# Output projection and gate as two passes over pairs of blocks, seven half-size products in place of eight

## The chip, the cores and the metric

The kernel runs as one program on one core of one Trainium2 chip. The metric is device time in microseconds (us), from the launch of the program to its end on that core; the kernel before takes 2761.39 us (median of three runs, 2760.68 to 2761.46). The names of the engines are those of the profile: PE is TensorE (PEld its weight loads), DVE is VectorE, ACT is ScalarE, POOL is GpSimd, and SP is SyncE, which only issues DMA transfers here.

## The reference, cut to what matters

One layer is computed for 2048 prompt tokens and for 64 sample tokens (8 sequences of 8), all in float32:

```python
xn   = rmsnorm(h, norm_mix)
proj = xn @ w_in + b_in                      # (tokens, 1024) @ (1024, 9 * 1024)
q, fz, iv, za, ga, gb, zb, ma, mb = split(proj)
o, s_new = hgrn2(silu(q), f(fz), iv, s0)     # recurrence with a 128 x 128 state for each of 8 heads
y_a  = (rmsnorm(o) * silu(za)) @ w_br_a
cv   = silu(layernorm(depthwise_conv31(ga * sigmoid(gb))))
y_b  = (cv * silu(zb)) @ w_br_b
merged = sigmoid(ma) * y_a + sigmoid(mb) * y_b
h    = h + merged @ w_o                                   # output projection
gate = sigmoid(rmsnorm(h, norm_ple) @ w_ple_gate)         # gate
h    = h + gate * (p_l @ w_ple)
y    = rmsnorm(h, norm_final)
```

The new recurrent states and the last 30 convolution inputs are outputs too. The change concerns mostly the four lines from `h = h + merged @ w_o` on. Both `w_o` and `w_ple_gate` are 1024 x 1024.

## The kernel before, in words

Each float32 matrix product is made of three products in a rounded type (`F32R`): an operand is split into a high part `hi`, which ACT makes with a copy into that type, and a low part `lo`, which DVE makes as `x - hi`; PE then adds up hi\*hi, hi\*lo and lo\*hi in PSUM. A tile of work for PE is one matmul with a 128 x 128 stationary operand and up to 512 moving columns.

There are three stages. The first (up to about 1980 us) goes head by head over two halves of the sequence: for each head the nine slices of `w_in` are multiplied by the transposed input (line 1374), and between those products PE works off the small matmuls of the recurrence. In the second half the sample tokens are a tail of the second prompt group. For each head, `sample_state` (line 611) multiplies the 64 transposed sample keys by a masked 64 x 1024 copy of the values `vm` in two matmuls of 512 columns in plain float32 (line 613), eight states of 128 x 128 in all. The second stage (about 1980 to 2324 us) is the two branch products, `w_br_a` and `w_br_b`, with the layer norm of the convolution between them on DVE, ACT and POOL. In these two stages an order written out by due times decides: `at_time(t, fn, prio)` puts a step behind the unit of PE work in whose time `t` falls; a unit is one product of 512 columns or less, with 24 matmuls.

The third stage (from about 2324 us) has no due times, only the order of the calls at the end of the kernel. It works block by block, 128 tokens each, 16 prompt blocks and one of 64 sample tokens (class `Out`, line 1163). For a block, `load_m` and `split_m` bring the transposed `merged` block and split it; `out_proj` (line 1215) makes two products of 24 matmuls (8 slices of the contraction times 3), adds the residual, squares and sums; `rstd` runs three short POOL instructions; DVE scales the block into `hs`; `turn` (line 1241) transposes it on PE and splits it; `gate` (line 1264) makes two products of 24 matmuls with `w_ple_gate` and two of 6 matmuls with `w_ple`, takes the sigmoid, multiplies, adds to `h`, squares again, and `L1287` scales the finished block, which ACT's queue stores. All matmuls of this stage are on line 1203, in `gemm`. The sample block packs its high and low parts side by side in the 128 stationary columns and so needs two matmuls where the others need three.

Both weights lie in SBUF split into high and low parts, `w_o` prepared by 16 loads and splits in the last part of the second stage, one half of `w_ple_gate` there too, the other half between the first blocks of the third stage. The call order is software-pipelined: `turn` of block b, `out_proj` of b+1, `split_m` of b+2, `gate` of b. The residual block `h` has three buffers; its load (line 1190) waits on SP until the output store of an older block has read its buffer, and the loads that are issued behind it on SP, `mgr` (line 1176) and `p` (line 1195), wait with it. This stage has eight PSUM buffers (`ps3`).

At the start, `x_load` brings the first two 128-token blocks, then the norm weights `nmix`, then the first weight slice; `x_norm` squares on ACT, computes the factor on POOL, and scales on DVE (line 166); `x_turn` transposes on PE (line 178) and splits.

## Time and profile before

| what | value |
|---|---|
| median of three runs | 2761.39 us |
| the profiled execution: time of the run, span from first to last instruction | 2761.78 us, 2760.0 us |
| mean granted TensorE clock | 0.999 |
| PE busy | 2735.6 us, 99% of the span |
| DVE, ACT, POOL busy | 1937.9, 928.7, 280.5 us |
| the chain that ended last, by engine | PE 95%, DVE 2%, DMA 1% |
| third stage, 2324 to 2760 us: PE, DVE, ACT, POOL busy | 427.12, 180.54, 133.52, 31.86 us |

The table is read from top to bottom: first whether the clock was full, then which engine was busy nearly all the time, then whether the chain that ended last agrees with it. A busy PE is not a PE at its peak, since the recorded durations of matmuls overlap: a matmul of 512 columns lasts about 390 ns in the records, but the next one starts 227 ns after it. The spacing is what counts in a sum.

### The profile page before, as it was taken

To read this page: it belongs to the slowest core of one execution; us is meant where nothing else is said; L and a number is where in the kernel's file an instruction comes from. 1 tells how busy PE (TensorE), PEld (TensorE's weight loads), DVE (VectorE), ACT (ScalarE), POOL (GpSimd) and SP (SyncE) were. 2 spreads that over 40 slices of the span, in tenths; PEclk is the share of its full clock that TensorE was granted. 3 is DMA by queue.
4 is the path that set the end of the run, shared out by engine and by line. 5 is a ranking of instruction groups with operands and counts; after the bars stand their busy time and mean duration, and the time that the engine had idled before them with its cause. 6 is when DMAs were issued, how large, how long until landed. Compare 5 with 4: busy or idle time off the path is not lost.

```text
span 2760.0 us, 50577 instructions
## 1 busy us (share of the span) xinstructions
PE 2735.6 (99%) x21199; PEld 2354.0 (85%) x21199; DVE 1937.9 (70%) x3219; ACT 928.7 (34%) x2096; POOL 280.5 (10%) x441
## 2 busy tenths in 40 slices
PE   8999999999999999999999999999999999999998
PEld 6888888888888898989889898989889888888887
DVE  6577877877768887686878778787977765444433
ACT  5333333333333423323233333233244332323322
POOL 2001000000000000010000000000036410000000
PEclk9999999999999999999999999999999999999999
DMA  4222222222222422121222222223687776322211
GB/s 125 62 73 81 76 82 81 88 89 68 75 66 65 131 69 82 58 81 58 77 73 80 70 65 77 62 86 103 193 274 219 235 249 212 102 71 70 71 50 40
DMA packets 330252, 275.37 MB, mean 100 GB/s; under 512 B 16474, under 2 KB 281787, under 8 KB 330024
## 3 DMA queue, kind: packets, MB, share of 16 engines
q1 hardware_dynamic: 265552, 192.44, 23.3%
q10 hardware_dynamic: 64200, 79.51, 8.4%
q8 instruction: 166, 2.72, 0.4%
q14 instruction: 62, 0.51, 0.1%
q0 software_dynamic: 272, 0.19, 0.0%
HBM read 192.60 MB, written 79.49 MB: 99 GB/s over the span
## 4 chain that ended last, share of the span: by engine, by line
PE 95%; DVE 2%; DMA 1%; ACT 0%; issue 0%; POOL 0%; DVEq 0%; POOLq 0%; SPq 0%; ACTq 0%
PE mm L1374 71%; PE ps L1203 14%; PE d32p L468 1%; PE ab L476 1%; PE o L565 1%; PE kv L538 1%; PE o L567 1%; DVE acc L717 1%; PE kvs L613 1%; PE vtr L401 1%; PE pt L1254 0%; PE ktr L526 0%; PE otr L591 0%; DMA raw<-in_w_br_a_dram 0%; PE d32p L454 0%; PE ab L468 0%
## 5 line engine op out<-in xcount | busy, mean ns | idle before, releaser
L717 DVE SCALAR_TENSOR_TENSOR acc<-u,cw,acc 128x512 f32<-128x512 f32 x960 | 743.5, 774 | 20.7
L1374 PE MATMUL mm<-x1h,whi 128*128 128x320 f32 (+2 forms) x2112 | 705.5, 334 | 0.0
L1374 PE MATMUL mm<-x1h,wlo 128*128 128x320 f32 (+2 forms) x2112 | 688.4, 326 | 0.0
L1374 PE MATMUL mm<-x1l,whi 128*128 128x320 f32 (+2 forms) x2112 | 688.1, 326 | 0.0
L1374 PE MATMUL mm<-x0h,whi 128*128 128x512 f32 (+1 forms) x1416 | 562.9, 398 | 0.4 <-ACT x0h L181 0.4
L1374 PE MATMUL mm<-x0l,whi 128*128 128x512 f32 (+1 forms) x1416 | 551.8, 390 | 1.5 <-DVE x0l L182 1.3
L1374 PE MATMUL mm<-x0h,wlo 128*128 128x512 f32 (+1 forms) x1416 | 551.7, 390 | 0.0
L1374 PEld LDWEIGHTS mm<-x1h,whi 128*128 128x128 f32 x2112 | 397.4, 188 | 33.8 <-ACT rp L382 4.5
L1374 PEld LDWEIGHTS mm<-x1h,wlo 128*128 128x128 f32 x2112 | 397.3, 188 | 28.2
L1374 PEld LDWEIGHTS mm<-x1l,whi 128*128 128x128 f32 x2112 | 397.1, 188 | 26.3
L333 DVE TENSOR_TENSOR wlo<-raw,whi 128x1024 fp32r<-128x1024 f32 x176 | 216.3, 1230 | 216.0 <-ACT whi L332 209.9
L1374 PEld LDWEIGHTS mm<-x0h,wlo 128*128 128x128 f32 x1416 | 266.5, 188 | 56.9 <-DVE wlo L333 0.4
L1374 PEld LDWEIGHTS mm<-x0h,whi 128*128 128x128 f32 x1416 | 267.1, 189 | 55.0 <-issue 1.2
L1374 PEld LDWEIGHTS mm<-x0l,whi 128*128 128x128 f32 x1416 | 267.0, 189 | 52.8 <-DVE x0l L182 2.2
L332 ACT ACTIVATE whi<-raw 128x1024 fp32r<-128x1024 f32 x176 | 186.1, 1057 | 101.2 <-DVE mal L909 34.3
L1203 PE MATMUL ps<-woh,mgi 128*128 128x512 f32 x528 | 168.4, 393 | 0.5 <-DVE mgi L1185 0.5
L429 DVE TENSOR_TENSOR rp<-rp 128x512 f32<-128x512 f32 (+1 forms) x224 | 156.7, 700 | 9.6
L442 DVE TENSOR_TENSOR lvl<-kq,rp 128x512 f32<-128x512 f32 (+2 forms) x224 | 146.6, 654 | 1.9
L1203 PEld LDWEIGHTS ps<-woh,mgi 128*128 128x128 f32 x528 | 99.1, 188 | 21.3 <-DVE mgi L1185 1.0
L800 ACT ACTIVATE sp<-mm,vcol 128x512 f32<-128x512 f32 (+2 forms) x120 | 73.0, 609 | 127.9 <-PE mm L1374 116.0
L576 POOL TENSOR_SCALAR ors<-oss 128x4 f32<-128x4 f32 (+1 forms) x40 | 11.1, 276 | 970.2 <-ACT on L574 970.2
L1203 PE MATMUL ps<-wol,mgi 128*128 128x512 f32 x272 | 106.1, 390 | 0.0
(253 smaller groups left out, 3153.0 us busy)
## 6 DMA issues: line engine op xcount, KB each, us to landing
raw<-in_w_in_dram SPq DMA_DIRECT2D x144, 512.0 KB, 4.0
gate<-am_dr SPq DMA_DIRECT2D x24, 512.0 KB, 5.0
xt<-in_x_prompt_dram SPq DMA_DIRECT2D x16, 512.0 KB, 5.0
g_dr<-gst ACTq DMA_DIRECT2D x32, 256.0 KB, 2.8
cv_dr<-acc ACTq DMA_DIRECT2D x32, 256.0 KB, 2.2
raw<-in_w_br_a_dram SPq DMA_DIRECT2D x16, 512.0 KB, 5.4
raw<-in_w_br_b_dram SPq DMA_DIRECT2D x16, 512.0 KB, 6.7
mgr<-mg_dr SPq DMA_DIRECT2D x16, 512.0 KB, 4.9
```

The lines of the kernel that those rows point to most:

```text
L332: nc.scalar.activation(out=b.hi, in_=b.raw, func=AF.Copy)
L333: nc.vector.tensor_tensor(out=b.lo, in0=b.raw, in1=f32(b.hi), op=ALU.subtract)
L401: nc.tensor.transpose(pt[:, P * c:P * (c + 1)], self.vt[:, P * c:P * (c + 1)], ident)
L429: nc.vector.tensor_tensor(out=io, in0=io, in1=tt, op=ALU.mult)
L442: nc.vector.tensor_tensor(out=o, in0=a, in1=b, op=ALU.mult)
L468: nc.tensor.matmul(dst[32 * b:32 * b + 32, c, s:s + 16], lhsT=kk[:, o:o + 32], rhs=lv[:, o:o + 32].rearrange("p (a e i) -> p a e i", e=2, ...
L476: nc.tensor.matmul(self.ab[o:o + h, c, o + h:o + 2 * h], lhsT=lv[:, P * c + o:P * c + o + h], rhs=lv[:, P * c + o + h:P * c + o + 2 * h], ...
L538: nc.tensor.matmul(self.kv[:, c, :], lhsT=self.kt[:, c, :], rhs=self.v[:, c, :], start=True, stop=True)
L717: nc.vector.scalar_tensor_tensor(out=self.acc, in0=self.u[:, i:i + G], scalar=w, in1=self.acc, op0=ALU.mult, op1=ALU.add)
L800: nc.scalar.activation(out=s[:, 0:n], in_=ps[:, 0:n], func=func, bias=bias(kind, j))
L1203: nc.tensor.matmul(ps, lhsT=a[:, k, :], rhs=c[:, k, s], start=(k == 0 and i == 0), stop=(k == kn - 1 and i == len(ops) - 1))
L1374: nc.tensor.matmul(ps[:, 0:u.n], lhsT=w[:, k, :], rhs=x[:, k, sl], start=(k == 0 and w is u.block.hi and x is xh), stop=(k == KB - 1 and w ...
```

## The change

The two 1024 x 1024 products of the third stage are computed from quarters. Two blocks form a pair, so that the left operand is a 2 x 2 grid of (128 tokens) x (512 of the contraction), the weight a 2 x 2 grid of 512 x 512 quarters, and the result a 2 x 2 grid of (128 tokens) x (512 columns). Seven products of 12 matmuls each (4 slices of the contraction times 3), over sums of quarters, replace the eight quarter products; the sums of the left side are made per pair, and their results are recombined. Because the gate's weights take the place of the output projection's in SBUF, the stage becomes two passes over eight pairs: the first stores `h` and the transposed normed block to DRAM (`h_dr`, `t_dr`), the second loads both. The `w_ple` products and all transposes keep their number. The sample tokens are handled once in each pass, behind the fourth pair, from the same quarters: 40 matmuls in place of 32 in the output projection, and 40 as before in the gate, with 8 for `w_ple`.

Sums of weight quarters are formed in the second stage by POOL (16 loads, 16 subtractions and 16 stores of 128 x 512 for each weight) and kept in DRAM (`ts_dr`). In the first stage the sample state is computed from rows of 32, and at the start `nmix` is loaded ahead of the second block.

```diff
 # start
     x_load(0)
+    nc.sync.dma_start(out=nmix, in_=norm_mix...)
     x_load(1)
-    nc.sync.dma_start(out=nmix, in_=norm_mix...)
...
-    x_norm(0)
-    x_norm(1)
+    x_stat(0)
+    x_stat(1)
+    x_scale(0)
+    split_hi(blocks[0])
+    x_scale(1)
...
 # sample state: vm is now 128 x 2 x 128, made by DVE from a transposed copy of the values in row tiles
         def sample_state(self, e):
-            kv = ps_1.tile([P, 4, P], F32, tag="kv", name="kvs")
-            nc.tensor.matmul(kv..., lhsT=self.kts, rhs=self.vm[:, 4 * e:4 * e + 4, :]..., start=True, stop=True)
-            s0 = self.s0[:, 4 * e:4 * e + 4, :]
-            nc.vector.tensor_tensor(out=s0, in0=s0, in1=kv, op=ALU.add)
+            kvs = [ps_1.tile([P, 4, P], F32, tag=tag, name="kvs") for tag in ("kv", "ab")]
+            for i, kv in enumerate(kvs):
+                r = slice(64 * e + 32 * i, 64 * e + 32 * i + 32)
+                nc.tensor.matmul(kv[:, 0:2, :], lhsT=self.kts[r], rhs=self.vm[r], start=True, stop=True)
+            for i, kv in enumerate(kvs):
+                s0 = self.s0[:, 4 * e + 2 * i:4 * e + 2 * i + 2, :]
+                nc.vector.tensor_tensor(out=s0, in0=s0, in1=kv[:, 0:2, :], op=ALU.add)
...
 # second stage: sums of weight quarters
+    def sums_load(w, k):
+        for op in QUARTERS:
+            sums[w, k, op] = t = p2["sb"].tile([P, G], F32, tag="ts", name="ts", bufs=8)
+            nc.sync.dma_start(out=t, in_=w_src(w, op, k))
+    def sums_make(w, k, i):
+        nc.gpsimd.tensor_tensor(out=out, in0=a, in1=b, op=ALU.subtract)
+        store(w_src(w, op, k), out, 1)
...
 # third stage
+    PRODUCTS = (("a11", "b11"), ("s2", "t2"), ("a12", "b21"), ("s3", "t3"), ("s1", "t1"), ("a22", "t4"), ("s4", "b22"))
+        def add(self, op):          # s1 to s4, sums of left quarters; s1, s3, s4 share one buffer
+            nc.gpsimd.tensor_tensor(out=out, in0=a, in1=b, op=f)
+        def split(self, op):
+            nc.scalar.activation(out=hi, in_=src, func=AF.Copy)
+            nc.vector.tensor_tensor(out=lo, in0=src, in1=f32(hi), op=ALU.subtract)
+        def product(self, i):       # 12 matmuls
+            for k in range(4):
+                for j, (a, b) in enumerate(((ah, bh), (ah, bl), (al, bh))):
+                    nc.tensor.matmul(ps, lhsT=a[:, k, :], rhs=b[:, k, :], ...)
+        def more(self, r, e, t):
+            nc.gpsimd.tensor_tensor(out=self.part(r, e), in0=self.part(r, e), in1=t, op=ALU.add)
+        def scale(self, r):
+            rs = rstd(self.ss[r], P)
+            nc.scalar.dma_start(out=h_dr[b * P:(b + 1) * P], in_=self.h[r])
+            nc.vector.tensor_scalar(out=self.hs[r], in0=self.h[r], scalar1=rs, scalar2=None, op0=ALU.mult)
+        def gate_sum(self, r, e, d, u):
+            nc.vector.tensor_tensor(out=g, in0=self.ps[d], in1=u, op=ALU.add)
+            nc.scalar.activation(out=g, in_=g, func=AF.Sigmoid)
+        def gate_use(self, r, e):
+            nc.vector.tensor_tensor(out=g, in0=self.pp[r, e], in1=g, op=ALU.mult)
+            nc.vector.tensor_tensor(out=h, in0=g, in1=h, op=ALU.add)
+            self.square(r, e, g)
+        def finish(self, r):
+            rs = rstd(self.ss[r], P)
+            nc.vector.scalar_tensor_tensor(out=h, in0=h, scalar=rs, in1=nfin[:, c], ...)
+            nc.scalar.dma_start(out=y_p[0, b * P:(b + 1) * P, c], in_=h)
+    def prepare(q, i):              # steps for the next pair behind product i of this one
+        for f, op in {0: ((q.split, "a11"),), 2: ((q.split, "a12"),), 3: ((q.add, "s3"),),
+                      4: ((q.split, "s3"), (q.add, "s1"), (q.add, "s2")), 5: ((q.split, "s2"), (q.split, "a22")),
+                      6: ((q.split, "s1"), (q.add, "s4"))}.get(i, ()):
+            f(op)
+    def first_pass(q, i):
+        if i == 0:   q.keep_p1(); q.more(0, 0, q.u["p1"])
+        elif i == 1: q.more(0, 1, q.sum_u(1, "p1", "u2"))
+        elif i == 2: q.close(0, 0, 2)
+        elif i == 3: t = q.sum_u(3, "u2", "u3"); q.more(1, 1, t); q.more(1, 0, t)
+        elif i == 4: q.close(1, 1, 4); ...
+        elif i == 5: q.close(1, 0, 5)
+        else:        q.scale(1); q.close(0, 1, 6)
+    def second_pass(q, i):
+        if i == 0:   q.keep_p1()
+        elif i == 1: q.sum_u(1, "p1", "u2")
+        elif i == 2: q.ple(0, 0); q.gate_sum(0, 0, 2, q.u["p1"])
+        elif i == 3: q.sum_u(3, "u2", "u3")
+        elif i == 4: q.ple(1, 1); q.gate_sum(1, 1, 4, q.u["u3"]); q.sum_u(4, "u2", "u2")
+        elif i == 5: q.ple(1, 0); q.gate_sum(1, 0, 5, q.u["u3"]); q.ple(0, 1)
+        else:        q.finish(1); q.gate_sum(0, 1, 6, q.u["u2"])
+    for n, q in enumerate(stages):          # stages: 8 pairs of the first pass, 8 of the second
+        if n < 14: at_step(n, 6, stages[n + 2].load_raw)
+        if nxt:
+            at_step(n + 1, 1, lambda q=nxt: q.split("s4"))
+            at_step(n, 3, lambda q=nxt: q.load_h(1))
+            at_step(n, 6, lambda q=nxt: q.load_h(0))
+        if n < 8:
+            at_step(n + 1, 1, lambda q=q: q.turn(1))
+            at_step(n + 1, 3, lambda q=q: q.turn(0))
+        else:
+            if n != 12: at_step(n - 1, 5, lambda q=q: q.load_p(0))
+            at_step(n, 0, lambda q=q: q.turn_p(0))
+            at_step(n, 0, lambda q=q: q.load_p(1))
+            at_step(n, 1, lambda q=q: q.turn_p(1))
+            if n < 15: at_step(n + 1, 0, lambda q=q: q.finish(0))
+    for i in range(6):              # 16 pieces of the gate's weights, through three buffers (tag "g")
+        for op, k in pieces[3 * i:3 * i + 3]:
+            at_step(7, i, lambda op=op, k=k: piece_load(op, k))
+        for op, k in pieces[3 * i:3 * i + 3]:
+            at_step(7, i + 1, lambda op=op, k=k: piece_split(op, k))
+    for n, q in enumerate(stages):
+        for i in range(7):
+            q.product(i)
+            if 0 < n < 9 and i == 0: stages[n - 1].scale(0)
+            (second_pass if q.gate else first_pass)(q, i)
+            if nxt: prepare(nxt, i)
+            if q.gate: second_use(q, i)     # gate_use of the product just summed, at i = 2, 4, 5, 6
+            for fn in extra.get(7 * n + i, ()): fn()
```

`r` is the row of the pair (its first or second block), `e` the half of the columns. `close` adds a product out of PSUM to `h` on DVE and squares on ACT; `sum_u` adds a product to a running sum on DVE. A step runs behind product i of pair n; `at_step(n, i, fn)` appends to it.

## Rows read from the trace of the kernel before

**Rows 1.** The page, part 1 (busy time) and part 4 (chain by line).

```profile
PE 2735.6 (99%) x21199; PEld 2354.0 (85%) x21199; DVE 1937.9 (70%) x3219; ACT 928.7 (34%) x2096; POOL 280.5 (10%) x441
...
PE mm L1374 71%; PE ps L1203 14%; PE d32p L468 1%; PE ab L476 1%; PE o L565 1%; PE kv L538 1%; PE o L567 1%; DVE acc L717 1%; PE kvs L613 1%; PE vtr L401 1%; PE pt L1254 0%; PE ktr L526 0%; PE otr L591 0%; DMA raw<-in_w_br_a_dram 0%; PE d32p L454 0%; PE ab L468 0%
```

**Rows 2.** Windows: stretch, its length, busy by engine (count), clock, DMA share, GB/s.

```profile
1980.00:2324.00 344.00, 343.23 (x1864) 301.73 (x1864) 242.75 (x428) 133.06 (x277) 113.76 (x146) 1.00 0.77 242
2324.00:2760.00 436.00, 427.12 (x1968) 354.38 (x1966) 180.54 (x331) 133.52 (x352) 31.86 (x102) 1.00 0.23 72
```

**Rows 3.** The chain of waits, third stage: start, length in us, what, matmuls.

```profile
2386.45 0.22 PE pt L1235 x2
2386.67 0.87 PE pt L1254 x8
2387.54 24.54 PE ps L1203 x108
...
2731.24 20.43 PE ps L1203 x90
```

**Rows 4.** Timeline of DVE, one block of the third stage: start, length, [idle before <-releaser].

```profile
2387.12 0.69 DVE L1277 TENSOR_TENSOR g<-ps,g 128x512 f32<-128x512 f32 x1 [5.33 <-ACT g L1276]
2387.84 0.69 DVE L1279 TENSOR_TENSOR h<-g,h 128x512 f32<-128x512 f32 x1
2390.57 1.29 DVE L1287 SCALAR_TENSOR_TENSOR h<-h,rs,nfin 128x1024 f32<-128x1024 f32 x1 [2.04 <-POOL rs L1304]
...
2401.24 0.75 DVE L1227 TENSOR_SCALAR hs<-h,rs 128x1024 f32<-128x1024 f32 x1 [2.04 <-POOL rs L1304]
```

**Rows 5.** Timeline of ACT, the same block.

```profile
2386.49 0.60 ACT L1276 ACTIVATE g<-ps 128x512 f32<-128x512 f32 x1 [3.86 <-PE ps L1203]
2388.63 0.63 ACT L1296 ACTIVATE junk<-h 128x512 f32<-128x512 f32 x1 [1.54 <-DVE h L1279]
...
2391.89 0.34 ACTq L1289 DMA_DIRECT2D out_dram<-h  x1
```

**Rows 6.** Late weight splits of the third stage, timelines of ACT and DVE.

```profile
2347.87 1.66 ACT L1400 ACTIVATE x1h<-bwr 128x512 fp32r<-128x512 f32 x3
2350.68 0.63 ACT L1400 ACTIVATE x1h<-bwr 128x512 fp32r<-128x512 f32 x1 [1.15 <-DMA bwr<-in_w_ple_gate_dram]
...
2349.87 2.49 DVE L1401 TENSOR_TENSOR x1l<-bwr,x1h 128x512 fp32r<-128x512 f32 x4
```

**Rows 7.** DMA issues, third stage: count, KB each, median us from issue to landing.

```profile
out_dram<-h ACTq DMA_DIRECT2D x15, 512.0 KB, 2.6
...
h<-in_x_prompt_dram SPq DMA_DIRECT2D x14, 512.0 KB, 3.5
bwr<-in_w_ple_gate_dram SPq DMA_DIRECT2D x8, 256.0 KB, 2.9
```

**Rows 8.** Line 1195, the loads of p (128 KB): issue to landing.

```profile
DMA to landing us min/median/max: 2.8/4.6/9.1
```

**Rows 9.** Waits of SP's queue, third stage: us in total, times, longest.

```profile
SPq L1190 <- DMA out_dram<-h: 300.3, 13, 24.2
```

**Rows 10.** Groups of POOL by shape: busy us, mean ns of one, idle before.

```profile
L997 POOL TENSOR_TENSOR sum<-sum,sq 128x256 f32<-128x256 f32 x49 | 40.0, 817 | 105.2 <-ACT sq L996 101.9
L609 POOL TENSOR_TENSOR s<-s,rp 128x1024 f32<-128x1024 f32 x8 | 17.4, 2179 | 194.2 <-PE os L603 194.2
L1041 POOL TENSOR_TENSOR cv<-cv,zb 128x320 f32<-128x320 f32 x8 | 8.1, 1047 | 7.2 <-DMA zb<-zb_dr 7.2
```

**Rows 11.** The chain of waits, first stage: small float32 matmuls.

```profile
56.78 0.39 PE d32p L454 x32
...
1940.35 0.22 PE o L567 x2
...
1944.42 1.05 PE kvs L613 x2
```

**Rows 12.** Timeline of DVE at the start: the first two blocks scaled.

```profile
8.68 2.48 DVE L166 SCALAR_TENSOR_TENSOR xt<-xt,xrs,nmix 128x1024 f32<-128x1024 f32 x2 [2.35 <-DMA nmix<-in_norm_mix_dram]
```

More of the change, by code (lines that the diff above doesn't have):

```diff
@@ L57 @@
 WGL = 1.6
+TS = (7.9, 8.7, 9.5, 10.3)
+TSG = (12.8, 13.5, 14.2, 14.9)
 MORE = 2
@@ new lines, in ple_gemm, with __init__ @@
+    def ple_gemm(lr, e, packed):
+        ps = ps3.tile([P, G], F32, tag="ps", name="pp")
+        ph, pl = lr
+        c = slice(G * e, G * (e + 1))
+        ops = ((ph, wph), (ph, wpl)) if packed else ((ph, wph), (ph, wpl), (pl, wph))
+        for k in range(2):
+            for i, (a, w) in enumerate(ops):
+                nc.tensor.matmul(
+                    ps, lhsT=a[:, k, :], rhs=w[:, k, c], start=(k == 0 and i == 0), stop=(k == 1 and i == len(ops) - 1))
+        return ps
+    class Sample:
+        def __init__(self, gate):
+            self.gate = gate
@@ L1308, in tile_hybrid_step, with finish @@
+        def finish(self):
+            rs = rstd(self.ss, NS)
+            nc.vector.scalar_tensor_tensor(
+                out=self.h[0:NS], in0=self.h[0:NS], scalar=rs, in1=nfin[0:NS], op0=ALU.mult, op1=ALU.mult)
+            nc.scalar.dma_start(out=y_s2, in_=self.h[0:NS])
+    pairs = [[Pair(i, g) for i in range(8)] for g in range(2)]
+    samples = [Sample(g) for g in range(2)]
     lns = [LnGroup(s, t0, n) for s, t0, n in (
@@ new lines, in tile_hybrid_step @@
+    nfin = p3.tile([P, D], F32, name="nfin")
+    at_step(7, 0, lambda: nc.sync.dma_start(
+        out=nfin, in_=norm_final.rearrange("(a d) -> a d", a=1).broadcast_to([P, D])))
+    b22_load(0, 0, 1, 2)
+    stages[0].load_h(1)
+    stages[0].load_h(0)
+    stages[1].load_raw()
+    stages[0].split("s1")
+    stages[0].add("s3")
+    stages[0].split("s3")
+    stages[0].add("s4")
+    stages[0].split("a22")
+    at_step(0, 0, lambda: stages[0].split("s4"))
+    at_step(0, 0, lambda: b22_split(0, 1, 2))
```

633 lines of the change are left out of this document (405 added, 228 removed).

## The prediction, on record before the result was known

> **What bounds the kernel now.** I read the page first. PE is busy for 99% of the span and every other engine for 70% or less, and the chain that ended last runs along PE's two matmul lines [rows 1]. The windows then say whether this holds in the stage that the change rewrites: from 2324 us on PE is busy for 427 of 436 us, DVE for 181, ACT for 134, POOL for 32, and the clock is full [rows 2]. Last I read the chain itself for the unit of the sum: one block is 108 matmuls in 24.54 us, that is 0.227 us a matmul, with 0.22 and 0.87 us of transposes, and the next block follows at once [rows 3]. So a matmul removed there is worth 0.227 us, but only as long as PE stays dense. That rests on the others keeping up, and it is what I have to check: the change gives them work that they don't have now and makes the operands of PE depend on longer loops.
>
> **Third stage, matmuls.** Before: 48 + 60 for each of 16 blocks and 72 for the sample, 1800. After: 84 for each of 8 pairs in the first pass, 84 + 24 in the second, and 40 + 48 for the sample, 672 + 864 + 88 = 1624. Saved: 176 x 0.227 = **40.0 us**. Transposes keep their number. A pair then costs PE 19.1 + 1.7 = 20.8 us in the first pass and 24.5 + 0.4 = 25.0 us in the second.
>
> **Second pass, a new loop.** I follow SP's queue. The load of the next pair's first block of h waits for the store of a finished block out of the same buffer; the trace shows this wait and what it holds: SP sat 300 us at 13 such loads [rows 9], harmless, since nothing behind them was urgent. Now the load of p for the second block stands behind it, and PE's transpose of that p stands ahead of the third product. The loop from the end of the sixth product of a pair: its last matmul runs out (0.16, a record of 0.39 less the spacing), DVE adds (0.69), ACT takes the sigmoid (0.60) and makes the next high part (0.63) [rows 4, 5], DVE makes two low parts (1.24, from 2.49 for four [rows 6]), multiplies and adds (0.73 + 0.69): 4.7. Then 2.04, in which DVE stands for the square and POOL's three instructions, and 1.29 for the scaling [rows 4]: 8.1. Then the store (2.6 to landing [rows 7]), 0.33 to issue the load of h, and 2.8 for p as the shortest of its landings [rows 8]: 13.8. PE meanwhile has two w_ple products, the seventh product, two products of the next pair and a transpose: 48 x 0.227 + 0.22 = 11.1. It stands 2.7 us. For seven pairs: **+19 us**. Bounds: 0, if PE finds p loaded after all; with the median landing of 4.6, 4.5 us a pair, +31. I take the low landing, because in the loads of 4.6 the 512 KB of mgr went ahead as well.
>
> **Change of pass.** The gate's 16 pieces of weights go through three buffers while the last pair of the first pass runs. One round of three is a load (2.9 [rows 7]), three copies on ACT (1.66 [rows 6]) and the low part of the last, about 5.2 us with its issue; 16 pieces are 5.3 rounds, 28 us. The steps they are tied to, six products and two transposes, last 18 us. ACT stands at pieces not yet landed, as it already did for 1.15 us with four buffers [rows 6]; behind it wait the high parts of the next pair, and on SP the load of p. I charge **+10 us**. Bounds: 0 (the loads run ahead of the copies and the slack of a pair hides the rest) and 25 (the lag also makes the wait of the loop above longer in the first two pairs of the second pass).
>
> **First pass.** PE's second product of a pair needs s2, which closes a loop of its own: POOL's sum s2, its split, the scaling of the last block, a square, the split of s1, sum s4, rstd, the scaling of the other block, three DVE steps and a square, the split of a12, a running sum, two additions to h and sum s3 on POOL, the split of s3, sum s1, and s2 again (s1, s3 and s4 share one buffer). These are six POOL additions of 128x512, 1.1 us of rstd (2.04 less the square and the handing over) and 12.2 us of DVE and ACT with 0.5 for handing over [rows 4 to 6]. No such POOL addition is in the trace; 256 columns take 0.82 and 1024 take 2.18 us [rows 10], by interpolation 512 take 1.27 (1.09 by proportion from the long one, 1.67 by proportion from the 320 columns at 1.05). I take 1.27, between its neighbours in size: 7.6 + 13.8 = 21.4 against PE's 20.8, 0.6 a pair, 4 in all, and 2 for the sample's split, which must wait for the sixth product's operand buffer: **+6 us**. Bounds: 0 at 1.09; 17 more at 1.67 (2.4 more on each of seven pairs).
>
> The Trainium skill, GPSIMD Engine Reference, 3.1 (Elementwise), has 4497 ns for an addition of 2048 columns; an estimate from that page alone is 1.12 us for 512, with which this term would be 2 and the time 4 us shorter. The rows decide, so 1.27 stays.
>
> **Sample state.** Eight heads with two matmuls of 512 columns, 1.05 us each: 16.8 us [rows 11]. A 128-column float32 matmul takes 0.22 us when it follows another (two in 0.22 are two records of one), so 512 take 0.88 and 0.17 is lost around them. After: 16 couples of 256 columns on different rows and PSUM banks. Side by side a couple takes 0.44 + 0.17 = 0.61, 9.8 in all; one after the other 1.05, no gain. No row shows row strips; the nearest is the column strips of 32, whose 32 records take 0.39 us where one after the other they would take 16 x 0.055 = 0.88 [rows 11], so they do overlap. I take side by side: -7.0, and +0.9 for eight more transposes of 0.11: **-6 us**. Bounds -6 and +1. DVE gets vm and one copy more a head, some 5 us in a stage in which it has gaps at the same heads; 0.
>
> **Start.** Scaling the first block waits 2.35 us, the last of it for nmix, and starts at 8.68 [rows 12]. With nmix second in the queue I take most of that, **-2 us**; bounds -4 (what follows on POOL and ACT moves up as well) and +1 (the second block lands later). Six short clears move on DVE behind the third unit, under PE's work on the fourth: 0, at most +2 if the first recurrence waits for them.
>
> **Weight sums in the second stage.** 32 POOL subtractions, some 41 us, where POOL is busy for 114 of 344, and 16.8 MB more at a DMA share of 0.77 [rows 2]. SP stands at the third group of loads until stores of the first have landed, and loads of the branch products stand behind it, but those run three units (16 us) ahead. 0; upper bound +5.
>
> **Tail.** Now 8.3 us follow PE's last matmul at 2751.7 [rows 3]. A sum and a sigmoid are added (1.3) and the earlier block's scaling is still in DVE's way (0.6): **+2 us**.
>
> **Sum.** -40 + 19 + 10 + 6 - 6 - 2 + 2 = -11 us. From the profiled execution's 2761.8 (span 2760.0, 1.8 around it) this is 2750.8; the median of the runs is 0.4 lower than that execution: **2750.4 us**.
>
> **Rivals.** *The second pass is dense.* For: SP issues far ahead of the calls, and a pair has 8 PSUM buffers of slack. Against: the store that the load waits for comes only after the scaling. Then the 19 go, and with a smooth change of pass 6 more: 2726.
>
> *The change of pass costs 25.* For: the four-buffer row already shows ACT standing. Against: half of the pieces could be early. 2765, no change.
>
> *POOL becomes the limit, and it is slower.* Place: the loop of the first pass. For: 320 columns took 1.05 us where 256 took 0.82 [rows 10], far more than in proportion, in the stage where DVE was busiest; and DVE will now be adding tensors all the time. Price: six additions more by 0.40 each on seven pairs, 17, and twelve low parts on POOL at the change of pass, 5: 2772, slower. It outweighs the gain from about 1.5 us an addition on. The Trainium skill, GPSIMD Engine Reference, 8 (Key points), has POOL share its SBUF interfaces with VectorE, with contention when VectorE reads two SBUF inputs; by that rule this rival would be the rule, and the 1.05 us agrees with it as far as one row can.
>
> *The row strips run one after the other*, so that this part doesn't do what it says: 2757. The Trainium skill, TensorEngine Tiling (Array Packing), Key Properties, says that tiles work independently, and that a change of tiling mode drains the engine; the first speaks against this rival, the second for it, and no run here shows either for row strips.
>
> **How the numbers follow.** Forecast 0.42 (own range 2741 to 2759), dense second pass 0.22 (2715 to 2741), costly change of pass 0.15 (2759 to 2770), slow POOL 0.17 (above 2767), row strips in sequence 0.04. About 0.2%, 5.5 us, is what a measurement of this kernel tells from no change. Faster than 2755.9: 0.36 of the forecast and 0.22, 0.58. Within: 0.06 + 0.04 + 0.11 = 0.21. Slower than 2766.9: 0.04 + 0.17 = 0.21. The range that leaves out 2 in 10 is 2726 to 2778.
>
> **What would show it.** PE's wait ahead of the p transposes (or of the w_ple product) of 2 to 4 us in each pair of the second pass, with SP's wait for the output store before it; without it the second term is wrong. The longest waits of PE in the whole stage at the first product or two of the second pass, released by ACT or a DMA. Pairs of the first pass 20.8 to 21.5 us apart; more means POOL. A 128x512 addition on POOL near 1.27 us. Two sample-state matmuls starting within 0.1 us of each other. First transpose before 8.5 us. The forecast is wrong if the second pass advances by 25 us a pair.

## The result, and the profile after

The changed kernel takes **2876.97 us** (median of four runs, 2876.15 to 2879.64) against 2761.03 us before on the same chip: a ratio of 1.0421, with a 95% interval of 1.0408 to 1.0435. It is 116 us slower; 2750.4 us had been predicted, in a range of 2726 to 2778.

The profiled execution has a span of 2874.5 us, 114.5 more than before. Page of the changed kernel, part 1 and the chain by engine (part 4), which answer to [rows 1]:

```profile
PE 2730.5 (95%) x21063; PEld 2343.7 (82%) x21063; DVE 2041.3 (71%) x3308; ACT 997.6 (35%) x2243; POOL 453.2 (16%) x573
...
PE 79%; DMA 6%; DVE 5%; POOL 4%; issue 3%; ACT 3%; SPq 0%; ACTq 0%; POOLq 0%; DVEq 0%
```

PE is no busier than before, but it holds only 79% of the chain that ended last instead of 95%: the work is strung together by transfers and by the other engines. The windows say where (the columns are those of [rows 2]). Second and third stage of the changed kernel:

```profile
1980.00:2352.00 372.00, 346.27 (x1828) 300.21 (x1827) 249.79 (x421) 133.30 (x279) 159.13 (x180) 0.96 0.84 268
2352.00:2875.00 523.00, 417.48 (x1795) 338.42 (x1793) 278.23 (x383) 200.51 (x489) 177.59 (x208) 0.89 0.41 137
```

The second stage ends at 2351.9 instead of some 2324 us, and the third takes 523 us instead of 436, with a granted clock of 0.89 where it had been 1.00. PE's waits in the third stage, which before hardly had any (us in all, times, longest):

```profile
PE pt L1410 <- DMA p<-in_p_prompt_dram: 64.8, 9, 16.0
PE ps L1305 <- ACT l_s L1283: 14.0, 3, 8.3
PE pp L1423 <- DVE x1h L1413: 8.4, 1, 8.4
PE ps L1455 <- DVE sl L1447: 3.5, 1, 3.5
PE pt L1391 <- DVE hs L1479: 2.0, 1, 2.0
```

With 2.1 us of smaller ones they come to 94.8 us. The whole difference can be added up. The last landmark of the first stage (the transposes `otr`) is 7.7 us earlier than before, at 1950.4. The first matmul of the third stage starts at 2351.85 instead of 2323.32, 28.5 us later, so the second stage lost 36.2. From there to PE's last matmul it is 512.5 us instead of 428.3; the 40.0 us of removed matmuls taken into account, 124.2 too many, of which 94.8 are waits. The other 29.4 are nearly all matmuls that ran slower: added up product by product, those behind waits took some 26 us more than 0.227 us each. Behind the last matmul stand 10.1 us instead of 8.3. Sum: -7.7 + 36.2 - 40.0 + 94.8 + 29.4 + 1.8 = +114.5.

What a slow matmul is can be seen behind any wait. PE in one pair of the second pass (start, length, what, [idle before <-releaser]), and the windows ahead of, in and behind that wait:

```profile
2655.71 3.02 PE L1305 MATMUL ps<-r_t,l_s 128*128 128x512 f32 x12
2662.33 0.62 PE L1410 MATMUL pt<-ident,p 128*128 128x128 f32 x2 [3.60 <-DMA p<-in_p_prompt_dram]
2662.60 4.52 PE L1305 MATMUL ps<-r_b,l_a 128*128 128x512 f32 x12
```
```profile
2650.10:2658.70 8.60, 8.60 (x39) 6.75 (x37) 5.31 (x8) 2.27 (x5) 1.10 (x4) 1.00 0.15 61
...
2662.30:2667.10 4.80, 4.77 (x15) 3.87 (x16) 3.68 (x6) 1.18 (x3) 0.54 (x1) 0.64 0.29 113
2667.10:2675.00 7.90, 7.90 (x37) 6.51 (x36) 4.39 (x7) 2.12 (x5) 0.75 (x1) 1.00 0.67 218
```

The same twelve matmuls take 3.02 us ahead of the wait and 4.52 behind it. The clock is 1.00 (2.4 GHz) before the pause and again from 2667 on; the mean of 0.64 in between mixes it with the lower level, 1.2 GHz. So this 3.6 us wait cost 5.1.

### The profile page after: what moved, and what is told of

It is laid out like the page before. It is cut to its first block, busy times and chain, and to the rows that moved or that the text cites. A ratio compares the mean times of both kernels' runs of the same rounds, so it can differ in the third digit from the quotient of the medians.

```text
span 2874.5 us, 51111 instructions
## 1 busy us (share of the span) xinstructions
PE 2730.5 (95%) x21063; PEld 2343.7 (82%) x21063; DVE 2041.3 (71%) x3308; ACT 997.6 (35%) x2243; POOL 453.2 (16%) x573
## 4 chain that ended last, share of the span: by engine, by line
PE 79%; DMA 6%; DVE 5%; POOL 4%; issue 3%; ACT 3%; SPq 0%; ACTq 0%; POOLq 0%; DVEq 0%
PE mm L1579 65%; PE ps L1305 3%; PE d32p L504 1%; PE ab L512 1%; POOL sf L1276 1%; PE kv L575 1%; PE o L602 1%; PE o L604 1%; POOL h L1324 1%; DMA ts_dr<-ts 1%; DMA p<-in_p_prompt_dram 1%; PE ps L1455 1%; PE pp L1423 1%; ACT l_s L1283 1%; POOL ts L1203 1%
## 5 line engine op out<-in xcount | busy, mean ns | idle before, releaser
L756 DVE SCALAR_TENSOR_TENSOR acc<-u,cw,acc 128x512 f32<-128x512 f32 x960 | 732.0, 762 | 20.7
L613 POOL TENSOR_SCALAR ors<-oss 128x4 f32<-128x4 f32 (+1 forms) x40 | 11.6, 289 | 1341.7 <-ACT on L611 1341.7
L1305 PE MATMUL ps<-r_t,l_s 128*128 128x512 f32 x384 | 102.4, 419 | 14.0 <-ACT l_s L1283 14.0
L1305 PE MATMUL ps<-r_b,l_a 128*128 128x512 f32 x384 | 105.0, 427 | 0.0
L1305 PEld LDWEIGHTS ps<-r_t,l_s 128*128 128x128 f32 x384 | 77.3, 204 | 32.3 <-ACT l_s L1283 15.2
```

What stands on the lines that cost most here:

```text
L756: nc.vector.scalar_tensor_tensor(out=self.acc, in0=self.u[:, i:i + G], scalar=w, in1=self.acc, op0=ALU.mult, op1=ALU.add)
L1305: nc.tensor.matmul(ps, lhsT=a[:, k, :], rhs=b[:, k, :], start=(k == 0 and j == 0), stop=(k == 3 and j == 2))
```

## The experiments

**The waits for p, and the matmuls behind them.** Each of the first kernels tests one suspect. Both loads of `p` go ahead of the load of `h`:

```diff
-                at_step(n - 1, 5, lambda q=q: q.load_p(0))
-            at_step(n, 0, lambda q=q: q.load_p(1))
+            for r in range(2):
+                at_step(6 if n == 8 else n - 1, 5, lambda q=q, r=r: q.load_p(r))
```

> Both loads of p of a pair are issued where the first one was, ahead of the load of h that waits for an output store (tiles: the second one lies in buffers that the second pass leaves idle; the sample's p is loaded ahead of its other tiles). Queue theory: the waits of PE at the p transposes (64.8 us in 9, and 8.4 at the sample's) go, and the slow matmuls behind them too; a pair of the second pass takes 25.0 to 25.8 us against 30.4, and the whole 2800 to 2825 us, more being left if the change of pass has a second cause. Rival, the recombination (DVE, ACT) is the limit of a pair: the wait moves to products of the pair, a pair stays above 28.5 us and the whole above 2855.

Measured: 2858.88 us, ratio to before 1.0353 (1.0337 to 1.0368), only 18 us better than the changed kernel. The rival was right (above 2855 us, a pair above 28.5), and the theory falls as far as the pairs are concerned. No p transpose waits any more, and the stretch from the sample's transpose to the second one of the next pair is 14 us shorter, but the three pairs behind the sample (from the second p transpose of the one to that of the other) still take 87.1 us instead of 87.8; PE alone would need 75.0. The wait stands two steps further on. All engines of p_early at the same place of a pair (three rows of others left out):

```profile
2660.39 1.28 DVE L1370 SCALAR_TENSOR_TENSOR h<-h,rs,nfin 128x1024 f32<-128x1024 f32 x1
2661.70 0.34 ACTq L1371 DMA_DIRECT2D out_dram<-h  x1
2662.09 0.38 ACT L1416 ACTIVATE x1h<-pt 128x256 fp32r<-128x256 f32 x1 [2.34 <-DVE h L1370]
...
2662.53 0.50 PE L1427 MATMUL pp<-x1h 128*128 128x512 f32 x1 [3.21 <-ACT x1h L1416]
```

Read from below: the `w_ple` product waits for the high part of p; ACT makes it late because it first has to issue the store of the other block, and that waits for DVE's scaling. The load on SP and this chain ended almost together, and the trace of the changed kernel named the later one.

> Adds 14 matmuls of 512 columns on resident weights ahead of the second p transpose of every pair of the second pass (112 in all, 25 us of PE), into the PSUM tile that the transposes then overwrite. Clock theory: PE stands there 3.6 us anyway, and without a pause the clock stays at its upper level: the 12 matmuls behind the wait take 2.9 us instead of 4.5, a pair 28.9 instead of 30.4, the whole 2863 to 2870. Rival, the slow matmuls wait for something else (weights, the split of p): they stay at 4.5 us, and the whole takes 2875 to 2880.

```diff
+        for i in range(14 * slot):
+            nc.tensor.matmul(pt..., lhsT=right["b11"][0][:, 0, 0:P], rhs=right["b11"][0][:, 1, :], start=True, stop=True)
         for i in range(2):
             nc.tensor.transpose(pt[:, i, 0:n], ...)
```

Measured: 2873.34 us (2872.17 to 2875.17), 3.6 less with 112 matmuls more; a gain of 0.1%, small, but the runs don't overlap with those of the changed kernel (2876.15 to 2879.64). The expected 2863 to 2870 is missed: the waits of the first pairs are longer than the 3.2 us of filling. Where it does fill, the twelve matmuls take 3.00 us, and the p transposes of successive pairs are 28.6 to 28.9 us apart, as expected, against 28.7 to 30.7. Windows of the same place in fill:

```profile
2649.60:2661.60 12.00, 11.74 (x53) 9.37 (x51) 6.93 (x9) 3.96 (x9) 2.97 (x7) 1.00 0.28 100
2661.60:2664.70 3.10, 3.04 (x15) 2.54 (x16) 2.23 (x3) 0.76 (x3) 0.19 (x1) 1.00 0.10 41
```

The clock stays at 1.00 and the same twelve matmuls are fast again, with nothing else about them changed: the slow ones were slow by the clock.

**The second stage.**

> Leaves out the sums of weight quarters in the second stage (32 loads, 32 subtractions on POOL, 32 stores); plain quarters are multiplied in their place, with the same loads later on, and two copies of 1 MB are made in the first stage for the two pieces read back from DRAM. Theory: the second stage loses its 35 us to the sums; the third stage starts near 2317 us instead of 2352 and the whole takes 2838 to 2849. Rival, the stage is late because of the late loads and sums for the first pair, not of the weight sums: under 10 us gained, above 2866.

```diff
-        r0 = (4 * w + int(op[1]) - 1) * G + P * k
-        return ts_dr[r0:r0 + P]
+        r, c = {"t1": (0, 1), "t2": (1, 0), "t3": (1, 1), "t4": (0, 0)}[op]
+        return (w_o, w_ple_gate)[w][0][G * r + P * k:G * r + P * (k + 1), G * c:G * (c + 1)]
...
-            at_time(t0 + dt - 0.3, lambda w=w, k=k: sums_load(w, k), 3)
-                at_time(t0 + dt + 0.8 + 0.2 * i, lambda w=w, k=k, i=i: sums_make(w, k, i), 3)
```

Measured: 2838.73 us; 38.2 come back, and the third stage starts at 2316.0, earlier than before the change. The sums, costed at nothing, lost as much as the change of pass (35.0 us of waits). PE's longest waits in the second stage of the changed kernel:

```profile
PE mu L1023 <- DVE sum L1016: 8.1, 1, 8.1
PE mm L1579 <- ACT x1h L1087: 6.1, 1, 6.1
PE rs L1066 <- POOL diag L1058: 3.1, 2, 2.6
```

PE waits at steps of the layer norm and at splits, but the longest wait begins with a weight. SP issues the load of a branch weight behind eight loads for the sums (issued from 1985.3 to 1998.4 us); it lands at 2008.9, ACT and DVE split it, and in DVE's queue the layer norm's sum, for which PE waits, stands behind that split. SP, ACT and DVE in the changed kernel, then the same split in no_sums, where PE waits 0.6 us:

```profile
2002.30 0.38 SPq L352 DMA_DIRECT2D raw<-in_w_br_a_dram  x1
2009.01 1.06 ACT L360 ACTIVATE whi<-raw 128x1024 fp32r<-128x1024 f32 x1 [19.82 <-DMA raw<-in_w_br_a_dram]
2010.10 1.23 DVE L364 TENSOR_TENSOR wlo<-raw,whi 128x1024 fp32r<-128x1024 f32 x1 [15.16 <-ACT whi L360]
2011.24 1.87 DVE L1016 TENSOR_REDUCE sum<-cv 128x128 f32<-128x1024 f32 x1
```
```profile
2002.68 1.23 DVE L364 TENSOR_TENSOR wlo<-raw,whi 128x1024 fp32r<-128x1024 f32 x1 [7.61 <-ACT whi L360]
```

The second longest runs through ACT's queue: the split that PE waits for stands behind two stores of sums, which ACT can issue only when POOL has subtracted (to 2267.8 us). The profile puts ACT's idle time down to an older transfer, but the stores end 0.05 us before the split begins:

```profile
2267.67 0.85 ACTq L383 DMA_DIRECT2D ts_dr<-ts  x2
2268.57 1.55 ACT L1087 ACTIVATE x1h<-cv 128x320 fp32r<-128x320 f32 x4 [13.41 <-DMA gate<-am_dr]
```

What part the queues have in this and what part the transfers, three kernels tried to tell:

> The 32 subtractions of weight quarters on POOL are left out, the 32 loads and 32 stores of the second stage stay (plain quarters are stored in place of the sums). Theory (what delays the second stage is SP's queue, with loads of weights standing behind loads that wait for a buffer, and the DMA engines at a share of 1.0): at least 25 of the 38 us stay, 2863 to 2877 us. Rival (POOL's 41 us in the way of the layer norm): 2840 to 2850 us.

```diff
-        nc.gpsimd.tensor_tensor(out=out, in0=a, in1=b, op=ALU.subtract)
         store(w_src(w, op, k), out, 1)
```

Measured: 2870.19 us, 6.8 better; the third stage starts at 2343.8. So 27.8 of the 35.9 us between no_sums and the changed kernel stay without any work on POOL: the transfers do it, or their places in the queues of SP (loads) and of ACT (stores).

> The changed kernel with the 32 loads for the weight sums issued by POOL's own queue instead of SP's (half a unit later in the order, with the same transfers, subtractions and stores). Theory (SP's order: loads of branch weights and of the layer norm stand behind loads that wait for a buffer): the loads of SP run ahead again, and of the 35 us lost in the second stage at least 20 come back: 2857 us or less. Rival (the 25 MB themselves, at a DMA share of 0.84 to 1.07, delay what PE needs): under 10 come back, 2867 us or more.

```diff
-            nc.sync.dma_start(out=t, in_=w_src(w, op, k))
+            nc.gpsimd.dma_start(out=t, in_=w_src(w, op, k))
```

Measured: 2885.28 us, slower still, with the third stage at 2360.0. SP no longer waits for buffers of the sums (28.6 us in the changed kernel), but POOL now does, ahead of its part of the layer norm (us in all, times, longest):

```profile
POOL ts L1197 <- DMA ts_dr<-ts: 44.6, 5, 29.8
```

SP's order had a part: the wait at the layer norm's first sum falls from 8.1 to 1.6 us. It isn't the whole cause, since others take its place; whether these come from the volume of the transfers (16.8 MB, not the 25 of the expectation; in the changed kernel the DMA share is 1.07 from 2020 to 2040 us), from the waiting at POOL or from the stores in ACT's queue, which all three kernels keep, is not shown.

> The same sums (32 loads, subtractions and stores) are made in the first stage, around 900 us, in tiles that are free there. Theory: PE has its operands far ahead there, POOL is busy for 5% and the DMA share is 0.26, so the sums cost nothing: as without them, 2837 to 2842 us. Rival (they cost wherever they stand, since POOL's additions slow DVE): 2850 us or more.

```diff
+    for n in range(8):
+        w, k = n // 4, n % 4
+        at_time(112 + 4 * n, lambda w=w, k=k: sums_load(w, k), 3)
...      # and the subtractions 2 to 5 units later; tiles of the first stage (tag "xt") in place of "ts"
```

Measured: 2846.60 us, 30.4 better, between the two forecasts. The second stage is whole again; its windows in sums_early:

```profile
1980.00:2323.00 343.00, 342.21 (x1860) 300.83 (x1859) 244.88 (x431) 134.26 (x280) 116.19 (x148) 1.00 0.77 244
```

The missing 8 us were lost in the first stage: its last landmark is at 1958.3, 7.9 us later than in the changed kernel. Moved a little earlier they cost next to nothing (1950.5 in rework, below, and 1950.7 to 1951.8 in the kernels built on it).

**The change of pass.**

> The p loads as in p_early; the 28 pieces of the gate's weights are neither loaded nor split, so that the second pass multiplies with the weights of the first (the gate's weights are left out). Theory (the change of pass is held by the pieces: SP's order, ACT, DVE and POOL): the waits between 2545 and 2635 us (10.3, 1.9, 8.7, 2.3, and slow matmuls) go but for some 5 us, and the whole takes 2825 to 2838 us against 2858.9. Rival (the turn from storing t and h to loading them holds it): under 8 us gained.

```diff
-            at_step(7, i, lambda op=op, k=k: piece_load(op, k))
-            at_step(7, i + 1, lambda op=op, k=k: piece_split(op, k))
...      # and the lists behind it: right_load, right_split, b22_load, b22_split
```

Measured: 2823.26 us, 35.6 less than p_early, as the theory said and 1.7 us beyond its range. Windows of p_early and of same_weights, the same 95 us:

```profile
2545.00:2640.00 95.00, 65.64 (x255) 51.13 (x254) 57.09 (x69) 45.53 (x106) 40.20 (x39) 0.82 0.56 198
```
```profile
2545.00:2640.00 95.00, 86.61 (x381) 69.93 (x379) 56.80 (x83) 39.59 (x96) 29.77 (x36) 0.96 0.42 152
```

In p_early no engine but PE is busy for more than 57 of the 95 us, and the DMA share is 0.56. That speaks for the order of the pieces, and against an engine without time for them, but the kernel takes away their loads and their splits together, so it doesn't separate the two. In p_early the chain runs through a load of h that waits 8.3 us for the store of its buffer, and through the loads of pieces that stand behind it on SP.

**The loop of the second pass.** Two more edits on top of p_early:

> The p loads as in p_early, and the stores of finished blocks are issued by SP instead of ACT (ACT's for the pair beside the sample). In p_early PE stood 29.7 us at w_ple products, for the high part of p on ACT, and ACT had stood 16.5 us at issuing an output store until DVE had scaled the block. Theory (ACT's queue in order is the second loop): ACT splits p when it is transposed, PE's waits at w_ple products fall below 5 us outside the change of pass, a pair takes 25.0 to 26.0 us against 28.6, and the whole 2836 to 2846 us. Rival (DVE's chain of sums, products and squares itself is the limit): the wait moves on to a product of the next pair or to DVE, a pair stays at 27.5 us or more, the whole above 2850.

> The p loads as in p_early (stores on ACT again), and one call moved: the scaling and store of a pair's first block, which stood ahead of the p transposes of the next pair, now stands behind both. Theory: no engine is full in the second pass; what holds a pair is one chain in the order of DVE's and ACT's queues, from the last product's sum over sigmoid, products, square, POOL's rstd and the scaling to the split of p. Without the scaling in it, p is split when it is transposed: PE's waits at w_ple products fall below 3 us outside the change of pass and the sample, a pair takes 25.0 to 25.8 us (28.6 in p_early, 27.6 in store_sp), and the whole 2836 to 2846 us. Rival (DVE's and ACT's work itself is too much): a pair stays at 27 us or more, above 2850.

```diff
 # store_sp
-                nc.scalar.dma_start(out=y_p[0, b * P:(b + 1) * P, c], in_=h)
+                (nc.scalar if self.i == 3 else nc.sync).dma_start(out=y_p[0, b * P:(b + 1) * P, c], in_=h)
 # finish_late
-                at_step(n + 1, 0, lambda q=q: q.finish(0))
+                finish0[n + 1] = q
+    for n, q in finish0.items():                           # behind turn_p(1)
+        at_step(n, 1, lambda q=q: q.finish(0))
```

Measured: 2853.15 and 2847.16 us. (The 28.6 us a pair that these expectations give for p_early was one pair; its others took up to 31.6.) The three pairs take 84.2 and 82.2 us. Both theories are missed (store_sp is as its rival said, finish_late between the two), and single pairs still take up to 31 us: each edit takes its wait away, and the next one, a little shorter, appears. In finish_late ACT splits p behind the square of the pair before. Then all repairs in one (the main lines of the edits):

> All repairs together: sums in the first stage (earlier than in sums_early), finish_late, the gate's weights loaded straight into their tiles as soon as a product of the last pair has freed them (two quarters by a copy made in the first stage) and split in place, the sample's products ahead of its w_ple products, its split in a tile of its own in the first pass, and the first h loads ahead of weight pieces. Theory: every part of the loss was an order of queues and none a lack of throughput; the third stage starts near 2317 us and takes 387 us of PE plus some 25 of leftovers, the whole 2735 to 2755 us, below the kernel before. Rival (the change of pass needs more of ACT, DVE and DMA than a pair has): 25 us or more of waits stay between the passes, the whole above 2762.

```diff
+    for i, op in enumerate(RIGHT[0:6]):               # whole quarters, straight into their tiles
+        at_step(7, max(i, 5) if op[0] == "t" and op in ("t1", "t4") else i, lambda op=op: right_load(1, op))
+    for i, op in ((3, "b11"), (4, "t2"), (5, "b21"), (6, "t3"), (7, "t1"), (8, "t4")):
+        at_step(7, i, lambda op=op: right_split(op))
...
+                self.pg = [self.gemm(i) for i in range(2)]     # the sample's products ahead of its w_ple products
```

> As rework, and the first p transpose of a pair, with its split, moved ahead of the sum of the last product of the pair before. In rework and finish_late ACT still split p behind the square of the pair before, and a pair took 26.4 to 27.9 us. Theory (order of ACT's and DVE's queues, no lack of throughput): outside the change of pass and the sample a pair takes 25.0 to 25.3 us, PE's waits at w_ple products fall to 1 us or less, and the whole takes 2764 to 2774 us. Rival (DVE is what a pair waits for, busy 42 of 60 us and slowed by POOL): 26.5 us or more a pair, above 2778.

```diff
-            at_step(n, 0, lambda q=q: q.turn_p(0))
+            if i == 6 and n != 11 and nxt and nxt.gate:        # right behind the last product
+                nxt.turn_p(0)
```

Measured: 2785.42 us and 2779.53 us, ratios 1.0092 (1.0075 to 1.0109) and 1.0069 (1.0054 to 1.0084): 97 us better than the changed kernel, and still slower than before. Both theories are missed, and both times lie where the rivals had them. In rework2 the three pairs take 83.2 us. PE's waits in its second pass, and the window that DVE's share is read from:

```profile
PE ps L1462 <- DVE sl L1454: 3.7, 1, 3.7
PE pp L1430 <- ACT x1h L1419: 3.1, 1, 3.1
PE pp L1430 <- DVE x1l L1420: 2.9, 4, 0.7
PE ps L1309 <- ACT l_s L1286: 2.4, 3, 0.8
```
```profile
2562.00:2777.00 215.00, 188.47 (x807) 148.97 (x805) 146.90 (x199) 72.42 (x161) 50.57 (x76) 0.96 0.30 107
```

No single wait is left that is worth much. DVE is busy for 147 of 215 us, more than any engine but PE. The last two kernels take work away instead:

> As rework2; in the second pass the seven additions of a pair on DVE that recombine the products are left out (three running sums and four sums ahead of the sigmoid, which reads PSUM instead), 4.8 us of DVE a pair. In rework2 the three pairs behind the sample take 83.2 us where PE alone needs 75.0, with DVE busy for 147 of 215 us. Theory (DVE's share of the recombination holds the pair): 75 to 78 us for the three pairs, the whole 2762 to 2769. Rival (POOL's sums of the left side, late themselves and slowing DVE): 80 us or more, the whole above 2773.

> As rework2; in the second pass the four sums of left quarters of a pair on POOL are left out (plain quarters are split and multiplied in their place), 5.5 us of POOL a pair. By the theory of no_recombine (DVE's own additions) the three pairs behind the sample stay at 81 us or more, and the whole above 2774. By its rival (POOL's sums, and DVE's additions of two SBUF operands at 1.28 us beside them against 0.69 alone) they take 75 to 78 us, the whole 2762 to 2769.

```diff
 # no_recombine
-            nc.vector.tensor_tensor(out=g, in0=self.ps[d], in1=u, op=ALU.add)
-            nc.scalar.activation(out=g, in_=g, func=AF.Sigmoid)
+            nc.scalar.activation(out=g, in_=self.ps[d], func=AF.Sigmoid)
-            q.sum_u(...)                                       # all three
 # no_left_sums
+            self.f[op] = a11 if self.gate else out
+            if self.gate:
+                return
             nc.gpsimd.tensor_tensor(out=out, in0=a, in1=b, op=f)
```

Measured: 2762.97 us (ratio 1.0007, 0.9998 to 1.0017) and 2760.67 us (1.0000, 0.9991 to 1.0009). Both come down by 17 to 19 us, and in both the last two pairs take 25.0 us each, which is PE alone (the three 78.7 and 80.2; the first of them still carries the sample). For no_recombine the theory's time held; for no_left_sums the theory (above 2774) failed, and the time is 1.3 us below its rival's range. Leaving out either brings these pairs down to PE's own time, so the two theories don't exclude each other: DVE's additions and POOL's sums both belong to what holds a pair. POOL's sums also slow DVE, and that share can be read; how much of the gain is that and how much their own 5.5 us a pair, these kernels don't separate. The addition to `h` in the gate, DVE's groups in rework2 and in no_left_sums:

```profile
L1364 DVE TENSOR_TENSOR h<-g,h 128x512 f32<-128x512 f32 x32 | 30.4, 950 | 3.1 <-DMA h<-h_dr 2.0
```
```profile
L1366 DVE TENSOR_TENSOR h<-g,h 128x512 f32<-128x512 f32 x32 | 22.1, 692 | 3.1 <-DMA h<-h_dr 2.0
```

One instance of each in the changed kernel, DVE and then POOL:

```profile
2646.83 1.28 DVE L1360 TENSOR_TENSOR h<-g,h 128x512 f32<-128x512 f32 x1
...
2651.93 0.69 DVE L1360 TENSOR_TENSOR h<-g,h 128x512 f32<-128x512 f32 x1
```
```profile
2646.27 1.29 POOL L1276 TENSOR_TENSOR sf<-mgr 128x512 f32<-128x512 f32 x1 [8.60 <-DVE l_s L1284]
2647.64 1.63 POOL L1276 TENSOR_TENSOR sf<-sf,mgr 128x512 f32<-128x512 f32 x1
```

DVE's addition takes 1.28 us where it starts during a POOL addition, 0.69 alone. The Trainium skill, GPSIMD Engine Reference, 8 (Key points), says that POOL shares its SBUF interfaces with VectorE, with contention where VectorE has two SBUF inputs; these rows agree. They also show who pays, namely the one that starts later: POOL's second addition, 1.63 us long, starts while DVE's first is under way. In the third stage of the changed kernel 14 of these 32 DVE additions start during a POOL addition and take 1.25 to 1.28 us; the other 18 take 0.69. Of the 85 POOL additions and subtractions of 512 columns that the timeline shows singly, 23 start during a DVE instruction that reads only SBUF, and 22 of these take 1.51 to 1.75 us; the other 62 take 1.26 to 1.31. DVE's additions with one operand in PSUM stay at 0.68 to 0.69 us beside POOL (42 cases).

**A version that beats both.**

> The kernel before with the first-stage parts of the change alone: row tiles for the sample state, and the first loads reordered. In the trace of the changed kernel the first landmarks are 1.7 us earlier and the last head's 7.7. Theory: PE is dense in the second and third stages of the kernel before, so all of it is kept: 2752.5 to 2754.5 us. Rival, given back at the first mean of the layer norm, which starts at 2013.1 us before and at 2013.2 after: 2759 to 2761.

Its edit is the first two parts of the diff above, on the kernel before. Measured: **2753.87 us** (ten runs, 2753.74 to 2754.64), ratio 0.9974 (0.9965 to 0.9984), a quarter of a percent, as the theory said. The 7.4 us that its first stage is shorter are worth 7.5 where PE is dense behind them; third stage of first_stage:

```profile
2316.00:2752.00 436.00, 427.36 (x1969) 354.48 (x1967) 180.88 (x332) 133.59 (x353) 31.70 (x102) 0.99 0.22 72
```

## Why the prediction was wrong

| term of the sum | predicted, us | measured, us |
|---|---|---|
| matmuls removed | -40 | -40.0 (worked out; the spacing of dense stretches is unchanged) |
| second pass, p loads | +19 | 18.2 of waits in five pairs; 20.0 more around the sample |
| change of pass | +10 | 35.0 of waits |
| first pass | +6 | 21.6 of waits, of another kind |
| sample state | -6 | -5.9 |
| start | -2 | -1.8 |
| weight sums | 0 (at most +5) | +36.2 |
| tail | +2 | +1.8 |
| lower clock behind waits | not in the sum | +29.4 (with small rests) |

**Right.** The matmuls, the sample state, the start and the tail, and the mechanism of the second pass: SP's wait at the load of h for the output store and the p load behind it are there as traced. The loop from the end of the sixth product to p's landing took 14.8 us (2647.6 to 2662.3) instead of 13.8, so a wait is 3.6 instead of 2.7. Two terms in it were short: p landed 3.3 us after its issue, not 2.8, and the addition to h took 1.28 us, not 0.69. That 18.2 us are so near to 19 is luck: there were five such waits and not seven, each a third longer. And this loop was not alone: without it (p_early) three pairs are 0.7 us shorter, because DVE's and ACT's chain ends almost as late. SP's waits in the third stage, which answer to [rows 9]:

```profile
SPq L1289 <- DMA out_dram<-h: 211.8, 13, 28.3
SPq L1289 <- DMA h_dr<-h: 118.3, 12, 16.6
```

A couple of row tiles holds PE for 0.64 us (from 1937.48 to the next start at 1938.12) where the matmul that it replaces held it for 1.05 [rows 11], and its two matmuls start within 0.02 us of each other, so they run side by side (0.61 predicted). The first transpose starts at 8.26 us, before the time at which the first block was scaled until then [rows 12]. POOL's additions of 512 columns take 1.26 to 1.31 us undisturbed and 1.36 on average (1.27 predicted from [rows 10]), and undisturbed pairs of the first pass are 20.9 us apart, so the rival of a slow POOL was rightly set aside as POOL's own limit. Its other half was missed: POOL and DVE slow each other. Two transposes of successive pairs in the first pass:

```profile
2523.05 0.82 PE L1391 MATMUL pt<-ident,hs 128*128 128x128 f32 x6
...
2543.92 0.82 PE L1391 MATMUL pt<-ident,hs 128*128 128x128 f32 x6
```

**Wrong:** four steps, the first by an overlap that did not hold, the second by size, the other two left out of the sum.

*"Weight sums in the second stage ... 0; upper bound +5."* The argument was that loads of the branch products run three units ahead. They did not: with 16.8 MB more the DMA share rose from 0.77 to 0.84 over the stage (1.07 from 2020 to 2040 us), and a branch weight landed so late that DVE, which had waited 7.3 us for its high part before the change, waited 15.2. What stood behind that weight in DVE's queue was the layer norm, of which the prediction asked nothing, and ACT's queue, which stores the sums, was not in it at all. no_sums gives 38 us back. A DMA share of 0.77 was no cover.

*Change of pass: "I charge +10 us. Bounds: 0 ... and 25".* The mechanism was right (pieces in rounds, ACT and SP behind them), the sum was not. It counted the 16 pieces that go through three buffers; 12 more are split behind them (`t1`, `t4` and `b22`, the 28 that same_weights leaves out). The lag went on into the third pair of the second pass (16.0, 11.6 and 7.5 us of waits), and the load of h for the new pass, waiting for a store, stood in SP's queue between the pieces. Taking the pieces away is worth 35.6 us.

*The sample tokens.* They were charged 2 us, in the first pass. In the second their p is split behind the whole gate of the pair ahead (8.4 us), and the next pair's p load stood on SP behind a wait for an output store (11.6): 20 us that no step of the prediction followed. In the first pass it was 3.5, 2.0 and, in part, a 4.8 us wait, whose chain also runs through a store of `h` and splits of `w_ple`; the largest there, 8.3 us, was POOL waiting for the stage's first load of h with the sums of the next pair behind it.

*The clock.* Every wait was priced at its own length. Of the five regular 3.5 to 3.9 us waits, four were followed by twelve matmuls in 4.5 to 4.6 us instead of 3.0. The Trainium skill, TensorE: Matmul & The Clock Gate, "HAM oscillation", describes this case, a wait for a transfer that comes in every round and makes each round start at half clock; the granted clock of 0.64 behind the wait agrees. Over the stage it is some 26 to 29 us, which alone would have turned the forecast into a loss.

The range ended at 2778 because each unknown was bounded by itself, from rows of a kernel in which PE never stood; the layer norm, the sample's second pass and the clock were not on the list and had no bound at all. By the forecast's own -11 us, the weight sums (36), the clock (29), the change of pass (25 more), the sample (20) and the first pass (16 more) make up the 126 us that were missing.

**What stays open:** in the second stage, how much the volume of the transfers does and how much their order on SP and ACT. A larger ring of tiles for the sums, and stores by another queue than ACT's, were not tried. Between the passes, rework2 still spends 52 us with 38 us of PE; what it would take to hide the rest was not found:

```profile
2510.00:2562.00 52.00, 38.03 (x150) 29.54 (x149) 37.47 (x42) 29.37 (x67) 27.33 (x24) 0.87 0.52 186
```

With all repairs and part of the work left out (no_left_sums), the third stage still takes 443 us from its first matmul against 437 before; that the whole kernel reaches the time before is owed to the first stage.

## What to carry to other kernels

Fewer matmuls are worth their time only while the engines that now recombine and split keep PE fed: count DVE's work between two products, with what it and POOL cost each other, before counting the matmuls saved. Where several queues in order meet in one loop, removing the wait that the profile names uncovers the next one (here the first removal shortened three pairs by 0.7 us); estimate the second-latest operand too. A recurring wait of PE can cost more than its length: behind four of the five regular ones twelve matmuls ran 1.5 us longer, at the lower clock. New transfers are not free because an engine's share is below 1: ask which queue issues them, and what stands behind them there.

## What was not expected of the hardware

- 112 extra matmuls that do nothing useful made the kernel 3.6 us (0.1%) faster: where they fill a wait of 3.5 us, the granted clock stays at 1.00.
- DVE's addition of two SBUF operands (128x512) takes 0.69 us alone and 1.25 to 1.28 us when it starts during a POOL addition; POOL's takes 1.26 to 1.31 us alone and, in 22 of 23 cases, 1.51 to 1.75 when it starts during such a DVE instruction. The later one pays.
- Two plain-float32 matmuls on row tiles of 32 partitions and 256 columns hold PE for 0.64 us as a couple, where one of 64 partitions and 512 columns held it for 1.05.
